# Two-layer hybrid trunk on one core: mLSTM scores formed once, gate products held back for its end, its norm split in two; RWKV's step output in another order; attention keys of two heads in one product

## The chip, the cores and the metric

The kernel runs on one core of one Trainium2 chip. The metric is device time in microseconds (us), the median of the runs shown; lower is better. Before the change it is 2833.07 us (three runs, 2829.2 to 2840.62). The core's engines run side by side, each through its own instructions in a fixed order: TensorE (PE in the rows, its weight loads PEld), VectorE (DVE), ScalarE (ACT), GpSimd (POOL) and SyncE (SP), whose queue issues the DMA transfers. The profile also gives the granted TensorE clock: 1.00 is the upper of its two levels (2.4 GHz), 0.50 the lower (1.2 GHz).

## The reference, cut to what matters

768 tokens (256 context, 512 latent) of width 1024 go through two layers. Each layer modulates its input, projects it, runs four mixers beside each other, merges them by gates, and ends in an MLP:

```python
y_ctx, y_lat = _merge(g, (a, b, c, d), w_branch, w_out)  # a mLSTM, b RWKV-7, c attention, d RG-LRU
gates = sigmoid(gate_u); y = einsum('btnm,nmd->btnd', o, w_branch); out = (sum_n gates*y) @ w_out
# mLSTM, each of two directions, chunks of 128 tokens, 4 heads of 64
qk  = einsum('bhnjd,bhnsd->bhnjs', q, k) * exp(log_d - m_j)       # only log_d, m_j differ by direction
num = einsum('bhnjs,bhnsd->bhnjd', qk, v) + s_prev * einsum('bhnjk,bhnkv->bhnjv', q, c_prev)
h   = num / maximum(abs(den), exp(-m_j));  out = _head_norm(h_fwd + h_bwd) * norm_g * sigmoid(o)
# RWKV-7: s_t = s_{t-1} (diag(w) - kk (kk*a)^T) + v k^T, y_t = s_t r_t, both directions
# attention: k_nope = ckv @ wuk (4 heads of 64), softmax over all keys
```

In the second layer only the 512 latent tokens are needed at the output; its states and keys still come from all 768.

## The kernel before

Activations lie transposed, 128 channels on the partitions and tokens along the row. The large products run as three products of split operands: `split` (L301 on ScalarE, L302 on VectorE) cuts a 512 KB weight block into `whi` and `wlo`, activations lie as `hhi`/`hlo`, and `mm3` forms hi*hi, hi*lo and lo*hi for each of eight blocks of 128 channels; all are written by `mm` (L388). One output block of an input projection is 24 products per token range: 256 and 512 tokens in layer 0, 512 alone in layer 1. Small products (scores, states, chunks of RWKV) run on plain fp32 operands, and the trace shows two records for each; transposes are L399, the 32x32 products L394.

The merge needs, for each of 4 branches (0 mLSTM, 1 RWKV, 2 attention, 3 RG-LRU) and each of 8 output blocks, a gate: one input-projection block and a tanh (`gate`, L661). A gate can be **parked**: formed early (`park`), stored to memory (`gd`, L928), and loaded again (L694) when `gates(n)` multiplies it with the branch's product `osp` x `wbr` (12 products in layer 0, 6 in layer 1; VectorE L701) and adds it on GpSimd (L705, not for branch 3, whose result is the first summand).

The order of the work is set in `mixers`: four generators (RWKV, the foreground RG-LRU, attention, mLSTM, then the gates of 3, 2 and 0; the filler, which parks gates; the modulation of the next blocks) are advanced in turns by a modelled time, in which each product has a cost and each yield a latency from the table PARM. What they issue is then laid out per engine when the program is built. `merge_last` forms the gates of branch 1 behind them, and `post` the output projection and the MLP.

The places of the change:
- `mlstm_pair` (L1197 to L1339), once for each two heads: projections, states (`pst`), then for d in two directions, load and exponentiate the decay matrices `mde` (POOL L1275, ACT L1279), form the scores `pS`, multiply (DVE L1290), form numerators `pn`, divide; and at the end the head norm over `hs` (DVE, ACT) and six transposes `pq<-cst,hs` (four in layer 1).
- `rwkv_step` (L1661 to L1713): 24 steps of both directions and both pairs of heads, 20 of them with an output `kpy`: for each of four (pair, direction) two products with the state `S` over 64 rows (tiles A and B, upper and lower half of the array), then one each with `SA` and `SB` over 128 rows.
- `mla` (L995 to L1103): the keys `kh` of each head, a 64-column product on `ckv`.
- `first_mod` and `layer` (L470 to L524): the first modulation blocks from `modw` at the start, and two weight blocks fetched ahead.

Of the kernel before, what the change touches and what calls it, by code (L numbers as in the profile page):

```python
# [13 lines left out]
AF = mybir.ActivationFunctionType  # L14
# [216 lines left out]
NF, NK, N4 = 16, 19, 6  # L231
NW = (3, 3)


# [11 lines left out]
class Trunk:  # L246
# [223 lines left out]
    def first_mod(self, quarters):  # L470
# [5 lines left out]
        for q in range(4):  # L476
            for i, (l, blk, _) in enumerate((units[q], units[4 + q])):
                end = (3, first - 1)[i]
                if q > end:
                    self.mod_unit(l, blk, q, first, 3)  # L480
                    continue
                for j in range(2):
                    raw = self.k4("modw")[:, 0:512]
                    nc.sync.dma_start(raw, self.ins["wmod"][l, blk, q, :, j, :])
                    self.mm(ps[i][0:2, :], lhsT=self.ccs[:, 2 * q + j, :], rhs=raw, start=(q + j == 0), stop=(q == end and j == 1))
                if q == end:
                    row = self.k4("modrow")[0:2, 0:512]
                    nc.scalar.activation(row, ps[i][0:2, :], AF.Copy)
                    pq = self.fp("pq")
                    for c in range(4):  # L490
                        self.mm(pq[:, 2 * c:2 * c + 2], lhsT=row[:, 128 * c:128 * c + 128], rhs=self.id2, start=True, stop=True)
                    self.add_mod(l, blk, pq, False)
# [8 lines left out]
    def layer(self, l):  # L501
# [4 lines left out]
        with ExitStack() as ctx:  # L506
# [3 lines left out]
            if l == 0:  # L510
                nc.sync.dma_start(self.vecs[0], self.ins["vec"][0])
                for part in range(2):
# [6 lines left out]
                    if part == 0:  # L519
                        self.ahead = {IP[i]: self.load_w(self.ins["win"][0, IP[i]]) for i in ("r0", "lru0")}  # L520
            self.derived()
# [77 lines left out]
    def mixers(self):  # L599
# [9 lines left out]
        self.parked = {}  # L609
        self.osplit = {}  # L610

        threads = [[self.rwkv(), 0.0, self.parm['hr']], [self.foreground(), 0.0, self.parm['hf']], [self.filler(), 0.0]]
# [23 lines left out]
    def foreground(self):  # L636
        yield from self.sec("lru", self.lru())
        yield from self.mla()
        yield from self.mlstm()
        for n, then in ((3, 2), (2, 0), (0, None)):  # L640
            yield from self.sec("ga", self.gates(n, then))

# [6 lines left out]
    def filler(self):  # L649
        for n in (3, 2, 0, 1):  # L650
            for dt in range(8):
                if (n, dt) not in self.parked and not (n == 1 and self.parm['left'] >> dt & 1 or n == 0 and self.parm['left0'] >> dt & 1):
                    self.park(n, dt)
                    yield self.parm["g3"] * (self.parm["g1"] if n == 1 else 1)

# [27 lines left out]
    def gates(self, n, then=None):  # L683
# [5 lines left out]
        for dt in range(8):  # L689
# [5 lines left out]
            else:  # L695
                self.parked[n, dt] = False
                th = self.gate(n, dt)
            ps, off = self.ps_for(R)
# [224 lines left out]
    def park(self, n, dt):  # L923

        self.parked[n, dt] = True
        th = self.gate(n, dt)
# [68 lines left out]
    def mla(self):  # L995
# [48 lines left out]
        for pair in range(2):  # L1044
            vt = f3("vt").rearrange("p (a b) -> p a b", b=128)
            for i0 in (0, 3):
# [4 lines left out]
                nc.scalar.activation(vt[:, i0:i0 + 3, :], pv[:, 0:384].rearrange("p (a b) -> p a b", b=128), AF.Copy)  # L1051
            qs, ks = [], []
            for e in range(2):
                h = 2 * pair + e
                ps, off = self.ps_full()
                self.mmf(ps[0:64], w1[:, 512 + 64 * h:576 + 64 * h], lambda a, b: ckv[:, a:b], W, off)
                kh = f3("kh")
                nc.scalar.activation(kh[0:64, :], ps[0:64, off:off + T], AF.Copy)
                nc.gpsimd.tensor_scalar(kh[64:96, :], kr[64:96, :], 1.0, 0.0, op0=ALU.mult, op1=ALU.add)
                ks.append(kh)  # L1060
                ps, off = self.ps_for(self.ranges(full))
# [135 lines left out]
    def mlstm_pair(self, pair, tk):  # L1197
# [5 lines left out]
        c0 = q0 // 128  # L1203
        fp = self.fp
        ps, off = self.inproj(f"mk{pair}", True)
        k = f3("mk")
# [30 lines left out]
        for d in range(2):  # L1237
# [25 lines left out]
            stb.append(sb)  # L1263
            yield self.parm['ml0' if pair == 0 else 'ml1']

        hs = f3("hs")
        groups = [(0, 3), (3, 6)] if full else [(2, 4), (4, 6)]
        c3 = lambda ap: ap.rearrange("p (c k) -> p c k", k=128)
        for d in range(2):
            des = []  # L1270
            for e in range(2):
                r = 2 * pair + e
                de = f3("mde")
                nc.sync.dma_start(de[:, q0:T], self.su[1, 32 * d + r:32 * d + r + 1, q0:T].to_broadcast([128, T - q0]))
                nc.gpsimd.tensor_tensor(c3(de)[:, c0:6], c3(de)[:, c0:6],  # L1275
                                        self.mml[:, d].unsqueeze(1).to_broadcast([128, 6 - c0, 128]), op=ALU.add)
                for ch in range(c0, 6):
                    n = slice(128 * ch, 128 * ch + 128)
                    nc.scalar.activation(de[:, n], de[:, n], AF.Exp, bias=tk[:, ch, 0, d, r:r + 1])  # L1279
                des.append(de)  # L1280
            for (ca, cb) in groups:
                n = cb - ca
                for e in range(2):
                    pS = fp("pS")
                    for i in range(n):
                        ch = ca + i
                        self.mm(pS[:, 128 * i:128 * i + 128], lhsT=k[64 * e:64 * e + 64, 128 * ch:128 * ch + 128],
                                rhs=q[64 * e:64 * e + 64, 128 * ch:128 * ch + 128], start=True, stop=True)
                    de = des[e][:, 128 * ca:128 * cb]
                    nc.vector.tensor_tensor(de, pS[:, 0:128 * n], de, op=ALU.mult)  # L1290
                pn = fp("pn")
                for i in range(n):
# [4 lines left out]
                    for e in range(2):  # L1297
                        self.mm(pn[:, o + 65 * e:o + 65 * e + 65], lhsT=des[e][:, 128 * ch:128 * ch + 128], rhs=vt[:, ch, e, :],
                                start=False, stop=(e == 1))
# [9 lines left out]
                else:  # L1309
# [3 lines left out]
                    nc.vector.tensor_tensor(dst, dst, h4, op=ALU.add)  # L1313
                yield self.parm['ml0' if pair == 0 else 'ml1']

        n = 12 - 2 * c0
        x3 = hs[:, q0:T].rearrange("p (g k) -> p g k", k=64)
# [9 lines left out]
        nc.vector.tensor_tensor(x3, x3, st1[:, 1, 0:n].unsqueeze(2).to_broadcast([128, n, 64]), op=ALU.mult)  # L1327
        nc.vector.tensor_scalar(so[:, q0:T], so[:, q0:T], self.dv("mngh", pair), self.dv("mngh", pair), op0=ALU.mult, op1=ALU.add)
        o = f3("oml")
        i = c0  # L1330
# [7 lines left out]
        self.store_o(0, pair, o)  # L1338
        yield self.parm['ml0' if pair == 0 else 'ml1']  # L1339

# [320 lines left out]
    def rwkv_step(self, u, pos, ci, y, S, need_y, written, last):  # L1661
# [33 lines left out]
        if need_y:  # L1695
            py = s4(kp("kpy"))
            for p, d in PD:
                n = at(p, d)
                o = py[:, p, d]
                for X in (A, B):  # L1700
                    self.mm(o[X], lhsT=S[X, p, d, :], rhs=u["KR"][X, n, 64:128], start=True, stop=False)
                self.mm(o[A], lhsT=WA[:, n, :], rhs=u["SA"][:, n, 64:128], start=False, stop=True)
                self.mm(o[B], lhsT=WB[:, n, :], rhs=u["SB"][:, n, 64:128], start=False, stop=True)
            for d in range(2):
# [24 lines left out]
```

## Time and profile before

| | before |
|---|---|
| median of three runs | 2833.07 us |
| the profiled execution, time / span | 2824.28 / 2822.5 us |
| PE / PEld busy | 2649.4 us (94%) / 2151.5 us (76%) |
| DVE / ACT / POOL busy | 1544.0 / 1029.3 / 444.4 us |
| mean granted clock | 0.963 |
| HBM traffic | 105 GB/s over the span |

The slices of the profile show PE busy nearly throughout; matmul ends are modelled, so a busy PE is one that has work in its pipeline. Layer 0's mixers lie at about 65 to 780 us, its merge and MLP up to about 1600, layer 1's mixers at about 1640 to 2285, its merge and MLP to the end. The granted clock is 1.00 in most slices and below it at the start, in two stretches (about 738 to 775 and 2267 to 2291 us) and at the very end, besides short dips.

### The profile page before, as it was taken

What the parts mean: (1) busy time and instruction counts of PE and PEld (TensorE: products, weight loads), DVE (VectorE), ACT (ScalarE), POOL (GpSimd) and SP (SyncE); (2) the same over time, 40 slices, a digit from 0 to 9 for tenths busy, and PEclk for the clock granted to TensorE, in tenths of its full rate; (3) what the DMA queues carried; (4) which work ended last, traced back from release to release, by engine and by line L of the source; (5) the groups of instructions that cost most, each with busy time, mean ns of one, the idle gap of its engine ahead of it and who ended that gap; (6) DMA issues with size and microseconds to landing.
All of it is one profiled execution on the core that took longest, in us unless ns stands there. A gap on an engine that the chain in (4) does not pass through costs nothing. (4 is left out here: it accounts for less than half of the span.)

```text
span 2822.5 us, 53833 instructions
## 1 busy us (share of the span) xinstructions
PE 2649.4 (94%) x23076; PEld 2151.5 (76%) x23076; DVE 1544.0 (55%) x2627; ACT 1029.3 (36%) x1642; POOL 444.4 (16%) x420
## 2 busy tenths in 40 slices
PE   7899999999899999999999988899999979999997
PEld 3777776778788877888888866666777857988887
DVE  5785766543324458655553575555564345843336
ACT  2554334333212235121212366543333323633325
POOL 0110112110103222010102200111211004211111
PEclk8999999999799999999999999999999989999999
DMA  6452321121244233434332242211212345333333
GB/s 234 144 174 80 103 94 43 36 92 66 97 149 160 93 113 105 127 121 127 119 127 76 91 134 89 88 50 54 62 58 80 123 131 185 129 112 97 97 97 105
DMA packets 119455, 300.89 MB, mean 107 GB/s; under 512 B 11264, under 2 KB 38272, under 8 KB 119216
## 3 DMA queue, kind: packets, MB, share of 16 engines
q1 hardware_dynamic: 119216, 297.44, 32.3%
q8 instruction: 181, 2.97, 0.4%
q14 instruction: 58, 0.48, 0.1%
HBM read 261.99 MB, written 35.31 MB: 105 GB/s over the span
## 5 line engine op out<-in xcount | busy, mean ns | idle before, releaser
L301 ACT ACTIVATE whi<-wraw 128x1024 fp32r<-128x1024 f32 x295 | 312.2, 1058 | 969.3 <-PE m L388 798.8
L388 PE MATMUL m<-hhi,whi 128*128 128x256 f32 (+1 forms) x2000 | 602.7, 362 | 22.2 <-ACT whi L301 8.1
L388 PE MATMUL m<-hlo,whi 128*128 128x256 f32 (+1 forms) x2000 | 593.5, 358 | 2.1 <-DVE hlo L907 1.9
L388 PE MATMUL m<-hhi,wlo 128*128 128x256 f32 (+1 forms) x2000 | 591.2, 357 | 0.9 <-DVE wlo L302 0.9
L302 DVE TENSOR_TENSOR wlo<-wraw,whi 128x1024 fp32r<-128x1024 f32 x291 | 364.7, 1254 | 401.1 <-ACT whi L301 395.7
L388 PEld LDWEIGHTS m<-hhi,whi 128*128 128x128 f32 x2000 | 381.0, 192 | 87.0 <-issue 8.8
L388 PEld LDWEIGHTS m<-hlo,whi 128*128 128x128 f32 x2000 | 383.3, 192 | 58.5 <-DVE hlo L907 4.9
L388 PEld LDWEIGHTS m<-hhi,wlo 128*128 128x128 f32 x2000 | 382.5, 192 | 55.9 <-issue 2.8
L459 DVE SCALAR_TENSOR_TENSOR modacc<-wraw,ccs,modacc 128x512 f32<-128x512 f32 x296 | 223.7, 804 | 39.6 <-DMA wraw<-wmod 39.5
L804 POOL TENSOR_TENSOR rl<-rl 128x512 f32<-128x512 f32 (+2 forms) x73 | 117.5, 1610 | 706.2 <-ACT rl L803 666.9
L388 PE MATMUL m<-fhi,whi 128*128 128x256 f32 (+1 forms) x608 | 175.9, 340 | 1.2 <-ACT fhi L301 1.2
L388 PE MATMUL m<-flo,whi 128*128 128x256 f32 (+1 forms) x608 | 175.4, 340 | 0.2 <-DVE flo L302 0.2
L388 PE MATMUL m<-fhi,wlo 128*128 128x256 f32 (+1 forms) x608 | 175.2, 339 | 0.0
L705 POOL TENSOR_TENSOR gth<-gth 128x768 f32<-128x768 f32 (+1 forms) x48 | 84.4, 1777 | 276.2 <-DVE gth L701 276.2
L388 PEld LDWEIGHTS m<-fhi,whi 128*128 128x128 f32 x608 | 113.9, 188 | 15.0 <-ACT fhi L301 1.4
L780 DVE SCALAR_TENSOR_TENSOR x<-m,dvec,x 128x512 f32<-128x512 f32 (+1 forms) x92 | 53.9, 607 | 129.9 <-PE m L388 129.8
L388 PEld LDWEIGHTS m<-flo,whi 128*128 128x128 f32 x608 | 114.3, 188 | 14.0 <-DVE flo L302 0.6
L388 PEld LDWEIGHTS m<-fhi,wlo 128*128 128x128 f32 x608 | 114.4, 188 | 13.5
L388 PE MATMUL m<-osp,whi 128*128 128x512 f32 (+1 forms) x384 | 103.3, 377 | 14.8 <-DVE gth L701 8.2
L302 DVE TENSOR_TENSOR flo<-rl,fhi 128x512 fp32r<-128x512 f32 (+2 forms) x73 | 55.2, 757 | 82.8 <-ACT fhi L301 82.8
L388 PEld LDWEIGHTS m<-osp,whi 128*128 128x128 f32 x384 | 70.0, 198 | 33.3 <-DVE gth L701 11.2
L301 ACT ACTIVATE fhi<-rl 128x512 fp32r<-128x512 f32 (+2 forms) x73 | 49.2, 673 | 112.4 <-POOL rl L804 112.4
(426 smaller groups left out, 4467.3 us busy)
## 6 DMA issues: line engine op xcount, KB each, us to landing
wraw<-wf SPq DMA_DIRECT2D x145, 512.0 KB, 3.5
wraw<-win SPq DMA_DIRECT2D x106, 512.0 KB, 3.9
wraw<-wmod SPq DMA_DIRECT2D x85, 512.0 KB, 3.6
wraw<-wout SPq DMA_DIRECT2D x28, 512.0 KB, 3.5
kwin<-rkv SPq DMA_DIRECT2D x20, 512.0 KB, 5.8
gd<-gth SPq DMA_DIRECT2D x24, 384.0 KB, 2.5
gth<-gd SPq DMA_DIRECT2D x24, 384.0 KB, 4.8
wraw<-wbr SPq DMA_DIRECT2D x16, 512.0 KB, 4.2
```

What stands on the lines that cost most here:

```text
L301: self.nc.scalar.activation(hi, src, AF.Copy)
L302: (self.nc.gpsimd if pool else self.nc.vector).tensor_tensor(lo, src, hi.bitcast(F32), op=ALU.subtract)
L388: self.nc.tensor.matmul(out, lhsT=lhsT, rhs=rhs, start=start, stop=stop)
L459: nc.vector.scalar_tensor_tensor(acc, w, c, acc, op0=ALU.mult, op1=ALU.add)
L705: nc.gpsimd.tensor_tensor(self.z[dt][:, q0:T], self.z[dt][:, q0:T], th[:, q0:T], op=ALU.add)
L780: nc.vector.scalar_tensor_tensor(x[et][:, a:b], ps[:, a + off:b + off], gm[:, et, j:j + 1], x[et][:, a:b], op0=ALU.mult, op1=ALU.add)
L804: nc.gpsimd.tensor_tensor(rl[:, a:b], rl[:, a:b], rl[:, a:b], op=ALU.mult)
```

## The change

1. **Scores once.** The decay matrices of both directions are made first (`des[d, e]`, four tiles in place of two at a time), the scores of a group of chunks are formed once and multiplied into both.
2. **Gates kept for mLSTM's end.** The filler stops when six gates are left (`NLATE`); `mlstm_pair` of the second two heads parks these itself, one after each direction's state, one after each group, two at its end (`late`).
3. **Norm in two parts.** The end of `mlstm_pair` becomes the generator `mlstm_tail`. For the last pair its first part (the norm) is issued ahead of the gates of branch 3, its second (transposes, output, store) after the third of these gates.
4. **RWKV's step output**: all eight 64-row products first, then the eight 128-row products.
5. **Keys of two heads** in one 128-column product; ScalarE copies each half.
6. **Start**: each `modw` block in one 512 KB transfer in place of two, and only `r0`'s weights fetched ahead, not `lru0`'s.

```diff
@@ first_mod / layer @@
+                raw = self.k4("modw", (128, 2, 512))
+                nc.sync.dma_start(raw, self.ins["wmod"][l, blk, q])
                 for j in range(2):
-                    raw = self.k4("modw")[:, 0:512]
-                    nc.sync.dma_start(raw, self.ins["wmod"][l, blk, q, :, j, :])
...
-     self.ahead = {IP[i]: self.load_w(self.ins["win"][0, IP[i]]) for i in ("r0", "lru0")}
+     self.ahead = {IP[i]: self.load_w(self.ins["win"][0, IP[i]]) for i in ("r0",)}
@@ foreground @@
+        tail = self.mlstm_tail(*self.ml_last)
+        next(tail)
         for n, then in ((3, 2), (2, 0), (0, None)):
-            yield from self.sec("ga", self.gates(n, then))
+            for dt, x in enumerate(self.sec("ga", self.gates(n, then))):
+                yield x
+                if n == 3 and dt == 2:
+                    for _ in tail:
+                        pass
@@ filler @@
+        while len(self.topark) > NLATE:
+            n, dt = self.topark[0]
+            self.park(n, dt)
+            yield self.parm["g3"] * (self.parm["g1"] if n == 1 else 1)
@@ mla @@
+            ps, off = self.ps_full()
+            self.mmf(ps, w1[:, 512 + 128 * pair:640 + 128 * pair], lambda a, b: ckv[:, a:b], W, off)
...
-                self.mmf(ps[0:64], w1[:, 512 + 64 * h:576 + 64 * h], lambda a, b: ckv[:, a:b], W, off)
@@ mlstm_pair @@
+        def late(n=1):
+            for _ in range(min(n, len(self.topark)) if pair else 0):
+                self.park(*self.topark[0])
...
+        for (ca, cb) in groups:
+            n = cb - ca
+            for e in range(2):
+                pS = fp("pS")
...
+                for d in range(2):
+                    de = des[d, e][:, 128 * ca:128 * cb]
                     nc.vector.tensor_tensor(de, pS[:, 0:128 * n], de, op=ALU.mult)
+            for d in range(2):
                 pn = fp("pn")
...
+            late()
+        if pair:
+            late(2)
+            self.ml_last = (pair, hs, so)
@@ rwkv_step @@
                 for X in (A, B):
-                    self.mm(o[X], lhsT=S[X, p, d, :], rhs=u["KR"][X, n, 64:128], start=True, stop=False)
-                self.mm(o[A], lhsT=WA[:, n, :], rhs=u["SA"][:, n, 64:128], start=False, stop=True)
-                self.mm(o[B], lhsT=WB[:, n, :], rhs=u["SB"][:, n, 64:128], start=False, stop=True)
+                    self.mm(o[X], lhsT=S[X, p, d, :], rhs=u["KR"][X, n, 64:128], start=(p + d == 0), stop=False)
+            for p, d in PD:
+                n = at(p, d)
+                o = py[:, p, d]
+                self.mm(o[A], lhsT=WA[:, n, :], rhs=u["SA"][:, n, 64:128], start=False, stop=(p + d == 2))
+                self.mm(o[B], lhsT=WB[:, n, :], rhs=u["SB"][:, n, 64:128], start=False, stop=(p + d == 2))
```

How the instructions lie now is shown at three places. The first is TensorE in an RWKV step of layer 0; `kps` is the state update ahead of the output, `po` attention's product behind it. Before:

```order
L388 MATMUL kps<-kWW,kBK 64x64 x7
L388 MATMUL kpy<-kKR,kS 64x64 x2
L388 MATMUL kpy<-kSA,kWW 64x64
L388 MATMUL kpy<-kSB,kWW 64x64
L388 MATMUL kpy<-kKR,kS 64x64 x2
```

And now:

```order
L389 MATMUL kps<-kWW,kBK 64x64 x7
L389 MATMUL kpy<-kKR,kS 64x64 x8
L389 MATMUL kpy<-kSA,kWW 64x64
L389 MATMUL kpy<-kSB,kWW 64x64
L389 MATMUL kpy<-kSA,kWW 64x64
```

The 64-row and the 128-row products alternated four times in a step; now each kind stands together.

The second is ScalarE at the end of the second pair of mLSTM in layer 0: `gth` is the tanh of a gate's product, `mde` the decay matrices, `msq` and `mhn` the norm, `osp` the split of branch 3's output for its gates. Before:

```order
L301 ACTIVATE whi<-wraw 128x1024
L1279 ACTIVATE mde<-mde,mtk 128x128 x12
L661 ACTIVATE gth<-m_7826 128x768
L1323 ACTIVATE msq<-hs 128x768
L1325 ACT_TABLE_LOAD
L1325 ACTIVATE mhn<-mhn,cbias 128x12
L1326 ACT_TABLE_LOAD
L1326 ACTIVATE mhn<-mhn 128x12
L301 ACTIVATE osp<-ot 128x768 x2
```

And now:

```order
L1299 ACTIVATE mde<-mde,mtk 128x128 x24
L302 ACTIVATE whi<-wraw 128x1024
L670 ACTIVATE gth<-m_7865 128x768
L302 ACTIVATE whi<-wraw 128x1024
L670 ACTIVATE gth<-m_7967 128x768
L302 ACTIVATE whi<-wraw 128x1024
L670 ACTIVATE gth<-m_8025 128x768
L302 ACTIVATE whi<-wraw 128x1024
L670 ACTIVATE gth<-m_8083 128x768
L1359 ACTIVATE msq<-hs 128x768
L1361 ACT_TABLE_LOAD
L1361 ACTIVATE mhn<-mhn,cbias 128x12
```

Behind the last decay matrices one gate's tanh came before the norm; now four do.

The third is SP's DMA queue where the gates of branch 3 begin, in layer 0: `gd` takes parked gates, `gth<-gd` brings them back, `ot` is a branch's output, `oml` mLSTM's. Before:

```order
L665 DMA od<-oml 128x768
L678 DMA ot<-od 128x768
L694 DMA gth<-gd 128x768 x3
L928 DMA gd<-gth 128x768
L342 DMA wraw<-wbr 128x1024
L694 DMA gth<-gd 128x768
```

And now:

```order
L687 DMA ot<-od 128x768
L940 DMA gd<-gth 128x768
L687 DMA ot<-od 128x768
L703 DMA gth<-gd 128x768 x3
L343 DMA wraw<-win 128x1024
L703 DMA gth<-gd 128x768
L674 DMA od<-oml 128x768
L703 DMA gth<-gd 128x768
L687 DMA ot<-od 128x768 x2
L703 DMA gth<-gd 128x768 x8
```

The second half of branch 3's output stood behind mLSTM's store; now it stands behind the store of the last parked gate, mLSTM's store has moved behind four gate loads, and the gate loads follow each other without parked stores between them.

## Rows read from the trace of the kernel before

**Rows 1.** The page: span and busy time of the engines.
```profile
span 2822.5 us, 53833 instructions
PE 2649.4 (94%) x23076; PEld 2151.5 (76%) x23076; DVE 1544.0 (55%) x2627; ACT 1029.3 (36%) x1642; POOL 444.4 (16%) x420
```

**Rows 2.** TensorE's waits: releaser, us in total, times, longest.
```profile
PE pq L399 <- DVE hs L1327: 19.2, 4, 9.2
...
PE m L388 <- DVE gth L701: 12.7, 7, 3.2
```

**Rows 3.** Stretches: PE, PEld, DVE, ACT, POOL busy us; clock; DMA.
```profile
737.60:775.20 37.60, 27.44 (x113) 25.17 (x113) 15.51 (x33) 9.10 (x20) 3.57 (x2) 0.50 0.21 68
775.20:782.00 6.80, 4.68 (x18) 3.74 (x17) 1.47 (x2) 0.84 (x1) 0.00 (x0) 0.75 0.67 223
2266.80:2290.70 23.90, 13.53 (x41) 9.83 (x41) 9.65 (x22) 5.33 (x8) 0.00 (x0) 0.50 0.31 107
```

**Rows 4.** Timeline, layer 0, end of mLSTM: start, us, instruction, idle before.
```profile
769.61 0.96 DVE L1327 TENSOR_TENSOR hs<-hs,mhn 128x768 f32<-128x768 f32 x1 [2.19 <-ACT mhn L1326]
...
770.72 1.51 PE L399 MATMUL pq<-cst,hs 128*128 128x128 f32 x6 [9.20 <-DVE hs L1327]
```

**Rows 5.** Stretches of the mixers ahead of mLSTM's ends, both layers.
```profile
120.00:736.00 616.00, 585.68 (x7720) 464.45 (x7719) 371.12 (x765) 240.63 (x455) 89.19 (x110) 0.98 0.28 91
1700.00:2266.00 566.00, 530.72 (x6880) 398.45 (x6879) 302.66 (x631) 243.40 (x438) 83.86 (x100) 0.96 0.24 75
```

**Rows 6.** Groups by form: records of scores and step outputs.
```profile
L388 PE MATMUL pS<-mq,mk 64*128 64x128 f32 x160 | 32.0, 343 | 1.6 <-DVE mde L1290 1.6
...
L388 PE MATMUL kpy<-kKR,kS 64*64 64x64 f32 x320 | 27.0, 247 | 0.0
```

**Rows 7.** TensorE's timeline: an RWKV step's end in layer 0.
```profile
291.48 0.68 PE L388 MATMUL kps<-kWW,kBK 128*64 128x64 f32 x14
292.09 0.33 PE L388 MATMUL kpy<-kKR,kS 64*64 64x64 f32 x4
...
292.62 0.33 PE L388 MATMUL kpy<-kKR,kS 64*64 64x64 f32 x4
...
294.10 1.15 PE L388 MATMUL po<-pt,vt 128*64 128x128 f32 x18
```

**Rows 8.** TensorE's timeline: scores beside an RWKV step, layer 0.
```profile
623.30 0.68 PE L388 MATMUL kpx<-kS,kKR 64*64 64x64 f32 x16
623.91 0.93 PE L388 MATMUL pS<-mq,mk 64*128 64x128 f32 x6
624.78 0.68 PE L388 MATMUL kpq<-kX,kVI 64*64 64x64 f32 x16
```

**Rows 9.** TensorE's timeline: the keys of one head.
```profile
436.43 1.50 PE L388 MATMUL m<-ckv,mlaw 128*64 128x256 f32 x4
```

**Rows 10.** Timeline, layer 0: gates one behind the other.
```profile
869.91 0.84 ACT L301 ACTIVATE osp<-ot 128x768 fp32r<-128x768 f32 x1 [4.26 <-DMA ot<-od]
...
870.78 0.96 DVE L302 TENSOR_TENSOR osp<-ot,osp 128x768 fp32r<-128x768 f32 x1 [3.50 <-ACT osp L301]
...
873.61 1.22 PE L388 MATMUL m<-osp,whi 128*128 128x256 f32 x4 [3.17 <-DVE gth L701]
...
875.75 2.39 DVE L302 TENSOR_TENSOR osp<-ot,osp 128x768 fp32r<-128x768 f32 x1 [1.14 <-ACT osp L301]
...
878.41 0.85 PE L388 MATMUL m<-osp,whi 128*128 128x256 f32 x4
...
879.08 8.19 POOL L705 TENSOR_TENSOR gth<-gth 128x768 f32<-128x768 f32 x4 [1.76 <-DVE gth L701]
...
880.49 0.85 PE L388 MATMUL m<-osp,whi 128*128 128x256 f32 x4
```

**Rows 11.** Stretch of rows 10 just behind the wait: clock.
```profile
874.00:878.00 4.00, 4.00 (x15) 3.44 (x15) 2.86 (x2) 1.91 (x2) 3.32 (x2) 0.57 0.90 365
```

**Rows 12.** Tile `ot`: from issue to landing.
```profile
DMA to landing us min/median/max: 3.3/3.3/4.1
```

**Rows 13.** GpSimd's timeline, layer 1: gates one behind the other.
```profile
2345.48 14.17 POOL L705 TENSOR_TENSOR gth<-gth 128x512 f32<-128x512 f32 x9 [1.23 <-DVE gth L701]
```

**Rows 14.** TensorE's timeline at the start: the second half of the input arrives.
```profile
53.69 0.61 PE L388 MATMUL m<-hhi,whi 128*128 128x256 f32 x2
```

More of the change, by code (lines that the diff above doesn't have):

```diff
@@ L232 @@
 NW = (3, 3)
+NLATE = 6
 PARM = (
@@ L481, in first_mod @@
                     continue
+                raw = self.k4("modw", (128, 2, 512))
+                nc.sync.dma_start(raw, self.ins["wmod"][l, blk, q])
                 for j in range(2):
-                    raw = self.k4("modw")[:, 0:512]
-                    nc.sync.dma_start(raw, self.ins["wmod"][l, blk, q, :, j, :])
-                    self.mm(ps[i][0:2, :], lhsT=self.ccs[:, 2 * q + j, :], rhs=raw, start=(q + j == 0), stop=(q == end and j == 1))
+                    self.mm(ps[i][0:2, :], lhsT=self.ccs[:, 2 * q + j, :], rhs=raw[:, j], start=(q + j == 0), stop=(q == end and j == 1))
                 if q == end:
@@ L610, in mixers @@
         self.osplit = {}
+        kept = lambda n, dt: n == 1 and self.parm['left'] >> dt & 1 or n == 0 and self.parm['left0'] >> dt & 1
+        self.topark = [(n, dt) for n in (3, 2, 0, 1) for dt in range(8) if not kept(n, dt)]
         threads = [[self.rwkv(), 0.0, self.parm['hr']], [self.foreground(), 0.0, self.parm['hf']], [self.filler(), 0.0]]
@@ L649, in filler @@
     def filler(self):
[L650 to L654, printed above, removed]
+        while len(self.topark) > NLATE:
+            n, dt = self.topark[0]
+            self.park(n, dt)
+            yield self.parm["g3"] * (self.parm["g1"] if n == 1 else 1)
     def gate(self, n, dt):
@@ L696, in gates @@
                 self.parked[n, dt] = False
+                if (n, dt) in self.topark:
+                    self.topark.remove((n, dt))
                 th = self.gate(n, dt)
@@ L923, in park @@
     def park(self, n, dt):
+        self.topark.remove((n, dt))
         self.parked[n, dt] = True
@@ L1052, in mla @@
             qs, ks = [], []
+            ps, off = self.ps_full()
+            self.mmf(ps, w1[:, 512 + 128 * pair:640 + 128 * pair], lambda a, b: ckv[:, a:b], W, off)
+            for e in range(2):
+                kh = f3("kh")
+                nc.scalar.activation(kh[0:64, :], ps[64 * e:64 * e + 64, off:off + T], AF.Copy)
+                nc.gpsimd.tensor_scalar(kh[64:96, :], kr[64:96, :], 1.0, 0.0, op0=ALU.mult, op1=ALU.add)
+                ks.append(kh)
             for e in range(2):
                 h = 2 * pair + e
-                ps, off = self.ps_full()
-                self.mmf(ps[0:64], w1[:, 512 + 64 * h:576 + 64 * h], lambda a, b: ckv[:, a:b], W, off)
[L1057 to L1060, printed above, removed]
                 ps, off = self.ps_for(self.ranges(full))
@@ L1268, in mlstm_pair @@
         c3 = lambda ap: ap.rearrange("p (c k) -> p c k", k=128)
+        des = {}
         for d in range(2):
-            des = []
             for e in range(2):
                 r = 2 * pair + e
-                de = f3("mde")
+                de = des[d, e] = f3("mde")
                 nc.sync.dma_start(de[:, q0:T], self.su[1, 32 * d + r:32 * d + r + 1, q0:T].to_broadcast([128, T - q0]))
@@ L1279, in mlstm_pair @@
                     nc.scalar.activation(de[:, n], de[:, n], AF.Exp, bias=tk[:, ch, 0, d, r:r + 1])
[L1280 to L1289, printed above, removed]
+        for (ca, cb) in groups:
+            n = cb - ca
+            for e in range(2):
+                pS = fp("pS")
+                for i in range(n):
+                    ch = ca + i
+                    self.mm(pS[:, 128 * i:128 * i + 128], lhsT=k[64 * e:64 * e + 64, 128 * ch:128 * ch + 128],
+                            rhs=q[64 * e:64 * e + 64, 128 * ch:128 * ch + 128], start=True, stop=True)
+                for d in range(2):
+                    de = des[d, e][:, 128 * ca:128 * cb]
                     nc.vector.tensor_tensor(de, pS[:, 0:128 * n], de, op=ALU.mult)
+            for d in range(2):
                 pn = fp("pn")
@@ L1297, in mlstm_pair @@
                     for e in range(2):
[L1298 removed]
+                        self.mm(pn[:, o + 65 * e:o + 65 * e + 65], lhsT=des[d, e][:, 128 * ch:128 * ch + 128], rhs=vt[:, ch, e, :],
                                 start=False, stop=(e == 1))
@@ L1314, in mlstm_pair, with mlstm_tail @@
                 yield self.parm['ml0' if pair == 0 else 'ml1']
+            late()
+        if pair:
+            late(2)
+            self.ml_last = (pair, hs, so)
+        else:
+            for _ in self.mlstm_tail(pair, hs, so):
+                pass
+            yield self.parm['ml0']
+    def mlstm_tail(self, pair, hs, so):
+        nc = self.nc
+        f3, fp = self.f, self.fp
+        q0 = 0 if self.full else 256
+        c0 = q0 // 128
         n = 12 - 2 * c0
@@ L1328, in mlstm_pair @@
         nc.vector.tensor_scalar(so[:, q0:T], so[:, q0:T], self.dv("mngh", pair), self.dv("mngh", pair), op0=ALU.mult, op1=ALU.add)
+        yield
         o = f3("oml")
@@ L1338, in mlstm_pair @@
         self.store_o(0, pair, o)
-        yield self.parm['ml0' if pair == 0 else 'ml1']
     def shifted(self, name, idx, dst, full=True):
```

## The prediction

> **What bounds the kernel now.** I read first the page's line of engines: TensorE is busy for 2649.4 of 2822.5 us, VectorE for 55%, the rest for less [rows 1]. So time goes only where TensorE's own instructions get fewer or quicker, where it stops waiting, or where its clock comes back up. Second, TensorE's waits by releaser: the largest that the change touches is `pq<-DVE hs`, 19.2 us in four waits [rows 2]; it stands at the end of mLSTM's second pair. Third, the windows around those ends [rows 3]: 37.6 us in layer 0 and 23.9 us in layer 1 in which the clock was 0.50, so the lower level, and TensorE had 27.44 and 13.53 us of work in its pipeline. The timeline shows the norm, written last on VectorE, and the transposes that waited 9.20 us for it [rows 4]. Fourth, the mixers ahead of those ends: busy 585.68 of 616 and 530.72 of 566 us, 95 and 94% [rows 5]. There TensorE sets the pace, and an instruction less is nearly its whole time less.
>
> **The tails (edits 2 and 3).** At the upper level the work of the three stretches would take 27.44 x 0.5 = 13.7, 4.68 x 0.75 = 3.5 and 13.53 x 0.5 = 6.8 us. What the stretches cost beyond that is 23.9 + 3.3 + 17.1 = 44.3 us [rows 3]. Is there enough work to fill them? A gate's twelve products pace at 880.49 - 878.41 = 2.08 us [rows 10]; a parked gate has eight input blocks where the gate's branch has two, so about 4 x 2.08 = 8.3 us in layer 0, and two thirds, 5.5 us, in layer 1. Six of them are 50 and 33 us, against idle times of 10.2 and 10.4 us. They are no new work, only work kept from earlier, where TensorE had other products to run. The transposes now follow three gates of branch 3 (6.2 us) besides the two last parks, against 9.20 us of waiting. I take the whole 44.3 as removed.
>
> What is late next is the first gate of branch 3. In the order, the second load of `ot` now stands behind the store of the last parked gate, which waits for that gate's tanh. From then to the first gate: landing 3.3 us [rows 12], ScalarE's and VectorE's halves of the split, 0.84 and 0.96 [rows 10], and a tanh of about the size of the first of these, together 5.9 us; some 2 us of it lie beside products already issued, so a wait of 4 us. Behind the 3.17 us wait that stands there now, the clock was 0.57 for 4 us [rows 11], 1.7 us lost. The issue is queued on SP, and behind it stand the gates' loads, in time since they are needed later. That is 5 to 6 us per layer; I take 10 for both. **Edits 2 and 3: -34 us.** Bounds: at best all 44; at worst only the waits of rows 2 go and 4 us come back, -15.
>
> **Scores once (1).** 160 records of `pS` become 80 [rows 6]. Six of them took 624.78 - 623.91 = 0.87 us [rows 8], so 80 x 0.145 = 11.6 us. The multiplications on VectorE keep their number.
>
> **Keys (5).** Of eight per-head products on `ckv` over all tokens, four are left, each of twice the columns; one took 1.50 us [rows 9] for 64 columns, and I take the wider one at the same time, since the tokens set the length. 4 x 1.50 = 6.0 us. If the wider one took twice as long, nothing would go.
>
> **RWKV's output (4).** 320 records, 16 in each of 20 steps [rows 6], plus as many on 128 rows. A step's output took from 292.09 to 294.10, 2.01 us, in four pieces of about 0.53 that each change between the two shapes [rows 7]. The same shapes standing alone are shown: 16 records of 64x64 (`kpx`) in 0.61 us [rows 8] and 14 of 128x64 (`kps`) in 292.09 - 291.48 = 0.61 [rows 7], so 16 in 0.70. Sum 1.31, saved 0.70; if the first of `kps` lies partly before its row, 0.79. Twenty steps: 14 to 16, taken as 15 us. That the alternation is what costs is inferred, not shown, hence a rival.
> The Trainium skill, TensorEngine Tiling (Array Packing), Gotcha 1: PSUM Pressure, says that different row tiles cannot access one PSUM bank at the same time. By it eight products in a row of upper and lower half, which go to one tile `py`, would run after one another, and the edit would save little, the third rival's result. `kpx` writes one tile from both halves in the same way, in 0.61 us [rows 8], which speaks against it here.
>
> Together 11.6 + 6.0 + 15 = 32.6 us, in stretches where TensorE is 94 to 95% busy. Some of it turns into waiting for the chains that run beside; I count nine tenths. **Edits 1, 4 and 5: -29 us**; bounds -35 (a little above the sum, by the higher output figure) and 0 (everything handed to other chains).
>
> **The start (6).** `lru0`'s 24 products on the first 256 tokens no longer fill the wait for the second half, whose own products begin at 53.69 us [rows 14]. At the pace above they are a third of 8.3, 2.8 us; at that of the row (0.305 each) 7.3. I take **+4**, bounds 0 (they find another hole) and +8. The halved number of `modw` transfers moves the same bytes; 0, within the same bounds.
>
> **The gates (from 2).** The gates of three branches now stand without parks between them, 16 in a row in layer 0 and 22 in layer 1. GpSimd's additions took 8.19 / 4 = 2.05 us each beside TensorE's 2.08 [rows 10]; in layer 1 14.17 / 9 = 1.57 [rows 13] beside two thirds of 2.08, 1.39. That is level in layer 0, and 0.18 us late per gate in layer 1, which the buffers take up at first. On the other side the parks between gates no longer break the run. **0**, bounds -5 and +12.
> The Trainium skill, SBUF — State Buffer, section "SBUF: two separate sides", says that VectorE with two inputs from SBUF and GpSimd lock each other out of a port that they share. A split of `osp` took 0.96 us alone and 2.39 beside GpSimd's additions [rows 10, 11], which agrees; by the rule eight such splits (two branches, two halves, two layers) would cost 8 x 1.43 = 11 us. TensorE ran on without a wait behind the one shown, so the sum has 0.
>
> **Sum:** -34 - 29 + 4 = -59 us. The profiled execution took 2824.28 us, so its like would take 2765; the median of the runs is 8.8 us above it, and the same step from the median gives 2774. I predict that.
>
> **Rivals.**
> *The mixers are set by chains beside TensorE (R1).* If the scores, keys and step outputs end in front of waits for VectorE or ScalarE, only the tails count: -34 + 4 = -30, 2803 us. For it: the steps of RWKV depend on each other through VectorE and ScalarE, and the order is fixed by modelled times. Against: the 95% [rows 5]. Chance 0.15.
> *The gates starve (R2).* Without parks between them the runs wait for GpSimd's buffers or loads. For it: 12.7 us of such waits already stand in seven places [rows 2], and GpSimd's pace is level with TensorE's or behind it. Price: 0.18 x 16 = 3 us in layer 1, and some four more starts of a run at 3.2 us of wait and 1.7 of low clock, 20 us: -59 + 23 = -36, 2797. Against: two gates can be loaded far ahead. Chance 0.12.
> *The output's new order gives nothing (R3).* The halves exclude each other, or the changes of shape cost nothing: 15 x 0.9 = 13.5 us less gain, 2787. Chance 0.05.
> *The stall moves ahead (R4, slower).* Four decay tiles must be ready before the first numerators: GpSimd takes 3.57 / 2 = 1.8 us each and ScalarE 9.10 / 20 = 0.46 per exponential [rows 3], so 4 x 1.8 + 6 x 0.46 = 9.9 us from the first where two tiles took 6.3. When the products between the scores and the first numerators are shorter than that, TensorE stops and the clock falls as in rows 3. Then the ends are not cured but moved (0 for -34), the first pairs get the like (+44), and the scores' gain goes: 44 - (6 + 15) x 0.9 + 4 = +29, 2862 us. Against: a parked gate of 8.3 or 5.5 us is issued nearby, and other generators' products. Chance 0.06.
>
> **How the numbers follow.** The forecast has 0.62; its own range is 2748 to 2798 (from -84, every term at its best bound, to -36, the tails at -15 and the start at +8). The range reaches over R1 and R2 to 2815 and down to 2742, and leaves out R4 and the far ends. A difference under 0.5%, 14 us, is no change for a measurement of this kernel, so faster means below 2819 and slower above 2847. Faster: 0.61 of the forecast, 0.12 of R1, 0.10 of R2, 0.05 of R3, 0.88. Same: 0.01, 0.03, 0.02 of these and 0.01 of R4, 0.07. Slower: R4's 0.05.
>
> **What would show it.** The two stretches at 0.50 gone and the transposes without a wait over 2 us; a step's output in 1.2 to 1.4 us; 80 records of `pS`; the mixers ahead of the tails shorter by about as much as their records. I am wrong if the tails' clock stays at 0.50, if a new stretch of low clock stands at the decay matrices (R4), if TensorE's busy share in the mixers falls by the time saved (R1), or if waits for `gth` or `ot` between gates sum to over 30 us (R2).

## The result, and the profile after

The changed kernel takes 2759.8 us against 2831.1, a ratio of 0.9736 (95% interval 0.9693 to 0.9778). One of the four runs behind this median took 13724 us, which no row explains; the ratio leaves it out, and the other three lie between 2753 and 2765 us. Timed once more beside later experiments the kernel took 2760.03 us, ratio 0.9775 (0.9750 to 0.9800), a little above the 0.970 to 0.976 expected of that timing. So it is 2.3 to 2.6% faster, some 70 us; 59 were forecast. Its profiled execution, which is set against that of [rows 1]:

```profile
span 2752.8 us, 53610 instructions
PE 2591.9 (94%) x22980; PEld 2116.0 (77%) x22980; DVE 1538.8 (56%) x2627; ACT 1030.2 (37%) x1642; POOL 445.6 (16%) x420
```

TensorE's busy time fell by 57.5 us, while its instructions fell only by the 80 records of the scores and the 16 of the keys. Part of the gain is the clock: its mean rose from 0.963 to 0.975, which is 2822.5 x 0.037 = 104 us lost at the lower level before and 2752.8 x 0.025 = 69 us now, 35 of the 70. In the trace of the second timing the mean is 0.972, 2758.2 x 0.028 = 77 us, so 27. These are upper estimates, since they count every us at the lower level as half lost, whether TensorE had work in it or not. The rest is work and waits.

Waits of TensorE in the changed kernel, to be held against [rows 2] (releaser, us in total, times, longest):

```profile
PE m L389 <- ACT osp L302: 10.1, 3, 4.6
...
PE pn L389 <- issue: 6.0, 2, 3.8
...
PE m L389 <- DVE gth L712: 4.8, 6, 1.4
...
PE pq L400 <- DVE hs L1363: 2.3, 1, 2.3
```

The transposes' 19.2 us have become 2.3, and the gates' 12.7 have become 4.8. Two waits of some size stand in their place: at the first gate of branch 3 (`osp`) and at the first numerators (`pn`). The stretches of layer 0 in which they stand (us, busy of TensorE, its loads, VectorE, ScalarE, GpSimd; clock, DMA share, GB/s), against the first two of [rows 3]:

```profile
725.00:740.00 15.00, 11.23 (x60) 10.40 (x60) 4.05 (x9) 7.03 (x20) 5.37 (x3) 0.78 0.36 105
...
765.00:775.00 10.00, 5.55 (x33) 4.62 (x31) 2.18 (x2) 4.73 (x6) 0.00 (x0) 0.96 0.56 180
775.00:785.00 10.00, 9.76 (x41) 7.92 (x42) 4.95 (x6) 2.31 (x4) 0.00 (x0) 0.70 0.60 222
```

At these ends no stretch at 0.50 is longer than 10 us, where [rows 3] has 38 and 24; each of the two waits is followed by 7 to 10 us of low clock.

Where the time went shows when the same instruction is put at its time in both traces. The first `kpz` (RWKV's first chunk) comes at 181 us instead of 194; from there to the transposes of mLSTM's first pair it takes 463 us instead of 471; from these to the first use of `zhi`, past the end of the mixers and the gates of layer 0, 290 instead of 313. In layer 1 the stretch from its first input product (`m<-hhi,whi`) to the first use of `zhi` takes 725 instead of 750. The rest of both layers is the same within 2 us. Single stretches carry the scatter of the clock: in the second trace of the changed kernel the first three are 184, 468 and 287. The stretch from `kpz` to the transposes, before and after:

```profile
194.00:666.00 472.00, 449.30 (x6879) 349.27 (x6880) 291.00 (x649) 180.03 (x372) 75.98 (x87) 0.97 0.25 79
```
```profile
181.00:644.00 463.00, 434.66 (x6869) 343.10 (x6870) 291.02 (x648) 181.18 (x373) 76.50 (x87) 0.98 0.26 80
```

TensorE's busy time fell by 14.6 us, the stretch by 9; the rest became idle time, 28.3 us instead of 22.7.

An RWKV step's output, against [rows 7]:

```profile
275.18 0.68 PE L389 MATMUL kps<-kWW,kBK 128*64 128x64 f32 x14
275.79 0.68 PE L389 MATMUL kpy<-kKR,kS 64*64 64x64 f32 x16
...
276.92 1.48 PE L389 MATMUL po<-pt,vt 128*64 128x128 f32 x24
```

276.92 - 275.79 = 1.13 us where it was 2.01. Over all steps the outputs take 24.5 us where they took 43.3. The groups by form, against [rows 6, 9]:

```profile
L389 PE MATMUL kpy<-kKR,kS 64*64 64x64 f32 x320 | 13.5, 224 | 0.0
L389 PE MATMUL pS<-mq,mk 64*128 64x128 f32 x80 | 13.4, 314 | 0.0
...
L389 PE MATMUL m<-ckv,mlaw 128*128 128x512 f32 x8 | 4.2, 605 | 0.0
```

The scores' 160 records and 32.0 us are 80 and 13.4. Eight key records of 512 columns take 605 ns each; before there were sixteen of 595, so a product twice as wide takes the same time.

### The profile page after: what moved, and what is told of

Read it like the earlier page. It is cut to its first block, busy times and chain, and to the rows that moved or that the text cites. A ratio compares the mean times of both kernels' runs of the same rounds, so it can differ in the third digit from the quotient of the medians.

```text
span 2752.8 us, 53610 instructions
## 1 busy us (share of the span) xinstructions
PE 2591.9 (94%) x22980; PEld 2116.0 (77%) x22980; DVE 1538.8 (56%) x2627; ACT 1030.2 (37%) x1642; POOL 445.6 (16%) x420
## 5 line engine op out<-in xcount | busy, mean ns | idle before, releaser
L389 PE MATMUL m<-osp,whi 128*128 128x512 f32 (+1 forms) x384 | 102.4, 374 | 17.3 <-ACT osp L302 10.1
```

Of the source, the lines that this page charges most:

```text
L389: self.nc.tensor.matmul(out, lhsT=lhsT, rhs=rhs, start=start, stop=stop)
```

## Experiments

Five rounds each. The runs of one kernel lie up to 21 us from their median and follow the granted clock (the kernel before: 2815 us at 0.968, 2847 at 0.954). The intervals of the ratios reach 6 to 12 us to either side, so differences of single edits are good to some 10 us, and the traces are used for the rest.

**The start as before.**

```diff
-                raw = self.k4("modw", (128, 2, 512))
-                nc.sync.dma_start(raw, self.ins["wmod"][l, blk, q])
                 for j in range(2):
+                    raw = self.k4("modw")[:, 0:512]
+                    nc.sync.dma_start(raw, self.ins["wmod"][l, blk, q, :, j, :])
...
-                        self.ahead = {IP[i]: self.load_w(self.ins["win"][0, IP[i]]) for i in ("r0",)}
+                        self.ahead = {IP[i]: self.load_w(self.ins["win"][0, IP[i]]) for i in ("r0", "lru0")}
```

> The changed kernel with the start as before (two transfers for each modw block, both weight blocks fetched ahead). Theory S: the trace of the changed kernel reaches the first kpz at 181 us instead of 194, so the start gained 13 us; undone, the kernel takes 2760 + 13 = 2773 us and the first kpz stands near 194. Rival, the prediction's own step: the start costs 4 us, so undone the kernel takes 2756 and the 13 us come from elsewhere.

2776.7 us, ratio 0.9798 (0.9771 to 0.9824): 17 us more than the changed kernel by the medians, 7 to 18 by the ratios to its two timings. The first `kpz` stands at 195 us again. The start gained, about 13 us by its trace; the rival falls. What happened shows between 20 and 40 us, first in the kernel before, then in the changed one:

```profile
20.00:40.00 20.00, 12.62 (x60) 4.03 (x59) 11.10 (x35) 8.76 (x11) 0.00 (x0) 0.72 0.56 204
```
```profile
20.00:40.00 20.00, 16.75 (x86) 7.95 (x86) 14.60 (x42) 7.80 (x10) 0.17 (x3) 0.83 1.00 391
```

The DMA engines were busy 56% of that stretch and are now busy throughout. The DMA queue of SyncE says where they stopped (start, us from the first issue to the last). Before:

```profile
16.32 1.01 SPq L342 DMA_DIRECT2D wraw<-win  x2
18.55 17.22 SPq L484 DMA_DIRECT2D modw<-wmod  x7
35.87 0.38 SPq L449 DMA_DIRECT2D wraw<-wmod  x1
```

And now:

```profile
12.81 0.33 SPq L343 DMA_DIRECT2D wraw<-win  x1
14.06 3.93 SPq L484 DMA_DIRECT2D modw<-wmod  x4
18.56 2.50 SPq L450 DMA_DIRECT2D wraw<-wmod  x2
```

Seven small issues took 17 us, with everything else queued behind them. They did not come evenly: six were out by 25 us, and the DMA engines were full until then; the seventh stood until 35.45 us. Parts of the stretch in the kernel before, the seventh issue, what SyncE's issues of line 484 waited for up to 45 us (us in total, times, longest), and TensorE:

```profile
20.00:25.00 5.00, 4.32 (x21) 1.62 (x21) 0.08 (x1) 0.59 (x1) 0.00 (x0) 0.92 1.02 395
...
30.00:35.00 5.00, 2.38 (x4) 0.71 (x5) 5.00 (x13) 4.21 (x5) 0.00 (x0) 0.50 0.00 2
```
```profile
35.45 0.33 SPq L484 DMA_DIRECT2D modw<-wmod  x1
```
```profile
SPq L484 <- PE pmod L388: 16.4, 13, 9.6
```
```profile
32.62 1.01 PE L388 MATMUL m<-hhi,whi 128*128 128x256 f32 x2 [6.70 <-ACT whi L301]
33.55 8.84 PE L388 MATMUL pmod<-modw,ccs 128*2 128x512 f32 x15
```

The seventh transfer needed a buffer that a product `pmod` had to free. These products stood on TensorE behind the first two of `r0`, which waited 6.70 us for their split weights, and in the meantime the queue ran dry: no transfers between 30 and 35 us.

**Each half of the start by itself, on the kernel before.**

```diff
+                raw = self.k4("modw", (128, 2, 512))
+                nc.sync.dma_start(raw, self.ins["wmod"][l, blk, q])
...
```

> The kernel before, with one edit: each modw block in one 512 KB transfer. Theory T: the transfers' number is what paced the first modulation blocks; most of the start's 13 us comes from it, 2820 us, and the first r0 product stands near 25 us instead of 32.6. Rival A: the order of the weights' loads is what counts, so this alone gives under 4 us, 2828 or more.

2826.1 us, ratio 0.9982 (0.9962 to 1.0001); first `kpz` at 188 us.

```diff
-                        self.ahead = {IP[i]: self.load_w(self.ins["win"][0, IP[i]]) for i in ("r0", "lru0")}
+                        self.ahead = {IP[i]: self.load_w(self.ins["win"][0, IP[i]]) for i in ("r0",)}
```

> The kernel before, with one edit: only r0's weights fetched ahead. Rival A (the weights' loads take the queue from the modulation's second half, and without lru0's block it is earlier): most of the 13 us, 2820. Theory T: nothing or the loss of 4 us that the prediction had, 2831 to 2837.

2820.5 us, ratio 0.9968 (0.9946 to 0.9991); first `kpz` at 183 us. Either edit brings the DMA share between 20 and 40 us to 0.99 or 1.02, so both loosen the same stop, and their gains overlap: with the larger transfers the same number of buffers holds twice the bytes, and without `lru0`'s load the order on TensorE changes, whose products `pmod` begin at 24.03 us there, ahead of those of `r0`. Neither theory stands alone. In both traces the 7 and 12 us gained at the start are gone again by the end of the first mixers, in stretches with more low clock than before (17 and 24 us of it lost from `kpz` to the transposes, where the kernel before had 12). That does not come with the earlier start: the changed kernel lost 10 and 17 us there in its two traces, and 20 to 21 with the start as before. With the lost clock taken off, the stretch is 460, 463 and 460 us in the kernel before and with the two edits, and the ratios of the runs, 5 and 9 us, are in keeping with the 7 and 12, though the first interval reaches 1.

**RWKV's output in the old order.**

```diff
-                    self.mm(o[X], lhsT=S[X, p, d, :], rhs=u["KR"][X, n, 64:128], start=(p + d == 0), stop=False)
-            for p, d in PD:
-                n = at(p, d)
-                o = py[:, p, d]
+                    self.mm(o[X], lhsT=S[X, p, d, :], rhs=u["KR"][X, n, 64:128], start=True, stop=False)
...
```

> The changed kernel with RWKV's step output in the old order. Theory H: TensorE's time in the step outputs goes back from 24.5 to 43.3 us (both read from the traces), but of these 18.8 us only about half come out at the end, since the mixers' other waits take the rest: 2769 us. Rival F: nine tenths, 2777 us. Rival N: nothing, 2760.

2775.4 us, ratio 0.9791 (0.9765 to 0.9818): 15 us more than the changed kernel by the medians, 5 to 16 by the ratios. The outputs take 43.9 us again, in pieces as in [rows 7]. By the medians and by the 19 us of TensorE's time N is out, though the interval overlaps with that of the changed kernel's second timing (0.9750 to 0.9800). What the new order saves is the change of shape between products. One row more of the step in [rows 7]:

```profile
292.35 0.27 PE L388 MATMUL kpy<-kSA,kWW 128*64 128x64 f32 x1
```

Four 64-row records begin at 292.09 us, four 128-row ones at 292.35 and the next 64-row ones at 292.62, so each four take 0.26 or 0.27 us, where four of sixteen standing together take 0.61 / 4 = 0.15 and 0.52 / 4 = 0.13. A change costs about the same in either direction, also where the next product begins a new sum, so it is not the adding to a sum just written. The median is nearer F than H, but the scatter leaves the two open.

**Scores per direction again.**

```diff
-                de = des[d, e] = f3("mde")
+                de = f3("mde")
...
-        for (ca, cb) in groups:
-            n = cb - ca
+                des.append(de)
+            for (ca, cb) in groups:
+                n = cb - ca
...
-                for d in range(2):
-                    de = des[d, e][:, 128 * ca:128 * cb]
-            for d in range(2):
+                    de = des[e][:, 128 * ca:128 * cb]
...
```

> The changed kernel with the scores formed once per direction again and two decay tiles at a time. The prediction's step: 11.6 us of scores come back, 0.9 of them at the end, 2770 us. Rival W: with only two decay tiles ahead of the first numerators, the waits of 3.8 and 2.2 us at these (with the low clock behind them some 12 us for both layers) go, so that the net is nothing, 2758 to 2762.

2777.9 us, ratio 0.9791 (0.9761 to 0.9820), 18 us more by the medians, 5 to 16 by the ratios. The prediction's 10 lies among these, though here too the interval overlaps with that of the second timing, and W's mechanism falls: the waits at the numerators do not go with the two-tile scheme (8.0 us in five, the longest 3.6).

**The end as before: a first try.**

```diff
-NLATE = 6
+NLATE = 0
...
-        tail = self.mlstm_tail(*self.ml_last)
-        next(tail)
...
-            self.ml_last = (pair, hs, so)
-        else:
-            for _ in self.mlstm_tail(pair, hs, so):
-                pass
-            yield self.parm['ml0']
+        for _ in self.mlstm_tail(pair, hs, so):
+            pass
+        yield self.parm['ml0' if pair == 0 else 'ml1']
```

> The changed kernel with the end of mLSTM as before: no gates kept (all parked by the filler), norm and transposes at once. The prediction's step: 34 us come back, 2794, and two stretches at clock 0.50 of 20 to 40 us stand at the ends. Rival P: the stretch only moves with the work and the end gains less, under 20 us, 2780 or less.

2761.8 us, ratio 0.9762 (0.9728 to 0.9796): no loss. The edit did less than its expectation says: the calls that park gates inside the pair were left in, and took gates from the filler, which had not finished. So it took away the split norm alone. The transposes wait 14.6 us again in three waits, and the products of `osp` wait 6.3 instead of 10.1.

**The end as before, in full.**

```diff
         def late(n=1):
+            return
```
with the last diff.

> The changed kernel without edits 2 and 3 altogether: no gate is parked inside mLSTM's second pair, all parks fall to the filler, which still has some when the gates of branch 3 begin, so that they lie among the gates as before; the norm and the transposes follow at once. The run that was to show this had left the calls that park gates in the pair, and came out at 2762 us, so what it took away, the split norm, is worth nothing by itself. Theory P (the parked gates inside the pair are what cured the ends): two stretches at clock 0.50 come back, with 9 and 8 us of waiting at the transposes, and the time is 2760 + 34 = 2794 us, by the prediction's own step. Rival K (with scores formed once the chain is short enough without them): under 2775.

2784.7 us, ratio 0.9854 (0.9833 to 0.9875), 25 us more than the changed kernel timed beside it, 22 by the ratios. Layer 0's end, with the wait of [rows 4] come back:

```profile
719.00:756.00 37.00, 22.45 (x107) 20.89 (x106) 14.44 (x34) 13.29 (x32) 7.13 (x4) 0.59 0.24 75
```
```profile
757.60 1.51 PE L400 MATMUL pq<-cst,hs 128*128 128x128 f32 x6 [9.21 <-DVE hs L1356]
```

In layer 1 the transposes wait 8.1 us again, and stretches at 0.50 of 37 and 17 us stand at the two ends. Theory P holds by its mechanism, with a smaller sum (25 for 34); K falls.

**The end in full, with the split norm kept.**

```diff
         def late(n=1):
+            return
-NLATE = 6
+NLATE = 0
```

> As the last, but with the norm in two parts as in the changed kernel: its first part ahead of the gates of branch 3, the transposes after three of these. Theory P: the transposes find their tile ready, but TensorE still stands without products through the decay matrices and the numerators; most of the loss is there, 2780 to 2790 us. Rival S (the split suffices): within 5 us of the changed kernel, 2755 to 2765.

2789.1 us, ratio 0.9870 (0.9842 to 0.9898), no better than without the split. The wait changed its place (start, us, instruction, idle before):

```profile
745.81 2.00 PE L389 MATMUL m<-osp,whi 128*128 128x256 f32 x5 [7.34 <-ACT osp L302]
```

P holds, S falls. The gates kept back are worth the whole of the end, the split nothing.

**Stores of parked gates issued from ScalarE.**

```diff
-        self.nc.sync.dma_start(self.gd[n, :, dt, q0:T], th[:, q0:T])
+        self.nc.scalar.dma_start(self.gd[n, :, dt, q0:T], th[:, q0:T])
```

> The changed kernel, with one edit: the stores of parked gates are issued from ScalarE, behind its own tanh, not from SyncE. Theory Q: in the changed kernel the decay loads and the second half of branch 3's output stand on SyncE's queue behind a late gate's store that waits for its tanh; with the stores off that queue the waits at the first numerators (3.8, 2.2 us) and at the first gate of branch 3 (4.6, 4.1 us) shrink to under 1 us each and their low clock goes: 20 us less, 2740. Rival L: the waits are set by how late the loads' own buffers come free; the time stays at 2760, or is worse by ScalarE's issue time.

2747.9 us, ratio 0.9705 (0.9673 to 0.9737). Half of Q: the wait at the numerators is gone, that at the first gate of branch 3 is the same 10.1 us in three. The first half is explained by SyncE's queue in the changed kernel:

```profile
719.62 0.33 SPq L940 DMA_DIRECT2D gd<-gth  x1
720.04 1.40 SPq L1294 DMA_DIRECT2D mde<-su  x3
```
and GpSimd, which adds the masks to the tiles that they bring (start, us, instruction, idle before):
```profile
715.51 1.84 POOL L1295 TENSOR_TENSOR mde<-mde,mml 128x768 f32<-128x768 f32 x1 [48.84 <-DMA mde<-su]
726.50 5.37 POOL L1295 TENSOR_TENSOR mde<-mde,mml 128x768 f32<-128x768 f32 x3 [9.15 <-PE m L389]
```

Three of the four decay loads left behind a late gate's store, 9 us after the first. The profile puts GpSimd's wait down to a product of TensorE; what came late was the loads, issued at 720 to 721 and 4.6 to 6.7 us on the way. The second half is not SyncE's. ScalarE in the same kernel:

```profile
783.94 0.83 ACT L1359 ACTIVATE msq<-hs 128x768 f32<-128x768 f32 x1
...
784.79 1.28 ACT L1361 ACT_TABLE_LOAD   x1
786.09 0.30 ACT L1361 ACTIVATE mhn<-mhn,cbias 128x12 f32<-128x12 f32 x1
786.30 0.83 ACT L302 ACTIVATE osp<-ot 128x768 fp32r<-128x768 f32 x1
```

SyncE's queue has both loads of `ot` well ahead:

```profile
776.74 1.16 SPq L687 DMA_DIRECT2D ot<-od  x2
```

Yet the split begins at 786.30: it stands behind the norm's square and a table load on ScalarE.

**The decay loads ahead of the second late gate, branch 3's split ahead of the last.**

```diff
-            late()
+            if d == 0:
+                late()
...
                 nc.sync.dma_start(de[:, q0:T], self.su[1, 32 * d + r:32 * d + r + 1, q0:T].to_broadcast([128, T - q0]))
+        late()
+        for d in range(2):
+            for e in range(2):
+                r = 2 * pair + e
+                de = des[d, e]
                 nc.gpsimd.tensor_tensor(c3(de)[:, c0:6], c3(de)[:, c0:6],
...
-            late(2)
+            late()
+            self.osplit[3] = self.branch_in(3)
+            late()
```

> The changed kernel, with two edits in the order of mLSTM's end: the four decay loads ahead of the second late gate, and branch 3's output loaded and split ahead of the last. Theory Q: the same four waits go, 2740 us, without a word changed on ScalarE. Rival L: they stay, 2760.

2749.4 us, ratio 0.9711 (0.9677 to 0.9745). The numerators wait 2.5 us in two, the gates of branch 3 1.4. About half of the 20 us that Q named came out.

**Both.**

> Both improvements together: decay loads and branch 3's output ahead of the late gates, and the stores of parked gates issued from ScalarE. Theory Q (both remove the same queue wait): no better than either, 2743 to 2750 us. Rival M: the two take away different waits and add up, 2737 or less.

2739.65 us, ratio 0.9678 (0.9653 to 0.9703): 3.2% under the kernel before, and clear of the changed kernel's interval beside it (0.9750 to 0.9800). Its ends in both layers:

```profile
726.00:778.00 52.00, 52.00 (x348) 45.88 (x347) 21.38 (x43) 17.13 (x37) 7.94 (x4) 1.00 0.39 136
2173.00:2220.00 47.00, 46.96 (x265) 38.51 (x265) 23.66 (x55) 16.98 (x35) 5.99 (x4) 1.00 0.50 155
```

In these stretches TensorE does not stop and the clock stays up. In the same trace the mixers of layer 0 up to the first transposes lost 31 us at the lower level, where the changed kernel's two traces lost 10 and 17; one trace does not show whether that is scatter. The time lies between Q's 2743 and M's 2737, and against either half alone the intervals overlap, so whether the two add up is not settled.

## Why the prediction was right, point by point

- **What bounds the kernel.** TensorE, as read from [rows 1, 5]: less of its work in the mixers shortened them, and work put into its pauses shortened the ends. But more of the saved work turned into waiting than the tenth that I counted. In layer 0's mixers TensorE's idle time rose from 22.7 to 28.3 us while its busy time fell by 14.6, which is R1's mechanism in part.
- **The tails, -34.** The mechanism held: gates kept back fill the ends, the clock stays up, the transposes wait 2.3 us in all. Undone they cost 22 to 25 us, so the term was about 10 too large, inside its bounds of 15 to 44. The wait at the first gate of branch 3 was forecast at 4 us per layer and is 4.6 and 4.1; but its reason was the wrong one. I had the second `ot` load behind a store on SyncE; the run with the stores elsewhere shows ScalarE's order, the norm ahead of the split. What I did not count are the 3.8 and 2.2 us at the first numerators, which is the mechanism of R4 at a small size: the decay tiles do come late, behind a store on SyncE's queue, but 10.0 us of products (718.1 to 728.1 us) stand between the scores and the wait in layer 0. I also counted the split of the norm and the gates as one edit; apart, the gates are worth all of it and the split nothing, since the wait only moves from the transposes to the split of `osp`.
- **The scores, 11.6 x 0.9.** 80 records went as forecast. TensorE's time in the scores fell by 18.6 us, more than 11.6, because a third of the 160 stood at the low clock, most of them at the ends (0.25 to 0.35 us a record, against 0.09 to 0.18 at the upper level). Undone: 18 us by the medians, 5 to 16 by the ratios.
- **The keys, 6.0 x 0.9.** The wide product takes the time of the narrow one; the key records fell from 8.2 + 5.2 to 4.2 + 2.5 us, 6.7. Not tried by themselves.
- **RWKV's output, 15 x 0.9.** 18.8 us of TensorE's time, a step at 1.13 to 1.23 us where 1.31 was forecast, since the 128-row products in pairs pace at 0.52 us for 16, not 0.70. Undone, 15 us by the medians, 5 to 16 by the ratios. R3 is out, as far as the scatter allows. The Trainium skill, TensorEngine Tiling (Array Packing), Gotcha 1: PSUM Pressure, was named for it: by its rule products of the upper and the lower half cannot use one PSUM bank at the same time. Here sixteen records of both halves into one tile take 0.61 us, as those of `kpx` do [rows 8], and the order that puts them together is the faster one; no run forms them in separate tiles.
- **The start, +4.** The step that failed. I weighed what `lru0`'s products had filled and took the transfers for the same bytes, so nothing. They are the same bytes, but one of the transfers stood 10 us on SyncE's queue for a buffer, with the rest behind it: transfers of twice the size and one weight load fewer let the engines run full, and the start takes 13 us less. The row that said it was in the trace, DMA share 0.56 in a stretch in which TensorE waited 6.7 us for weights.
- **The gates, 0.** They no longer wait for each other: 12.7 us became 4.8. GpSimd's additions run at 8.12 us for four in layer 0 and 12.94 for eight in layer 1, the pace of [rows 10, 13], and R2 did not come.
- **The sum.** By the runs that undo one edit each: start 13 (by its trace), output 15, scores 18, ends 25, together 71 by the medians, and some 20 less if the output and the scores are taken at the low end of their ratios; the keys were not tried. That the forecast's 59 was near is in part luck: two errors went against each other, 17 us too little at the start and 10 too much at the ends. R1 came only in part, since the output and the scores both cost time when undone.

## What to carry to other kernels

Look at the issuing queue whenever a change touches transfers, also when the bytes stay the same: an issue that waits, for its buffer or for the data it is to store, held every load behind it here (10 us at the start, 9 us at the decay loads), and the profile put the late additions down to a product of TensorE, not to the queue. When work is kept back to fill a pause, follow each engine's order through the new end, and move the loads and splits that come after the pause ahead of the work that fills it. When two edits aim at one wait, undo each by itself, since here one of them was worth nothing.

## What was not expected of the hardware

- Changing between 64-row and 128-row products was dear here: a step's output with seven changes took 2.01 to 2.11 us, with one 1.13 to 1.23. That is some 0.9 us for six changes, 0.15 each, if all of it is put on them.
- 27 to 35 of the 70 us gained are clock, as an upper estimate: 104 us were lost at the lower level before, 69 and 77 in two traces now.
- Between 20 and 40 us the DMA engines were busy for 0.56 of the time, for 0.99 to 1.02 with larger transfers or one weight load fewer. The size of a transfer is not the reason: from 20 to 25 us the transfers of 256 KB kept them at 1.02. One issue that waited for a buffer left them without work.
